# Triangular inverses in blocks of 16 instead of 8, with a planner that counts float32 products as two passes and new orders in both mixers

## The chip, the core and the metric

The kernel runs on one core of a Trainium2 chip. The metric is the device time of one execution in microseconds (us); the time quoted is the median of three runs.

## The reference, cut to what matters

The kernel computes a trunk of two layers on 512 tokens of width 1024. Each layer is a half-step SwiGLU feed-forward, a mixer, and another half-step feed-forward, each with a norm before and after.

```python
def macaron_layer(x, mixer, ...):
    x = x + 0.5 * rmsnorm(swiglu(rmsnorm(x, ffn1_pre_g), ffn1_w_in, ffn1_w_out), ffn1_post_g)
    x = x + rmsnorm(mixer(rmsnorm(x, mix_pre_g)), mix_post_g)
    x = x + 0.5 * rmsnorm(swiglu(rmsnorm(x, ffn2_pre_g), ffn2_w_in, ffn2_w_out), ffn2_post_g)
    return x

def rwkv7_step(S, inp):              # mixer of layer 0, 8 heads of 64, token by token
    r_t, w_t, k_t, v_t, kk_t, a_t = inp
    sa = einsum("bhvk,bhk->bhv", S, -kk_t)
    S = S * w_t[:, :, None, :] + einsum("bhv,bhk->bhvk", sa, kk_t * a_t) + einsum("bhv,bhk->bhvk", v_t, k_t)
    return S, einsum("bhvk,bhk->bhv", S, r_t)

# beside it in the same mixer: a gated linear recurrence h = a*h + u over 512 channels (RG-LRU)
# mixer of layer 1: stick-breaking attention, 16 heads of 64, blocks of 128 queries
```

## The kernel before

Activations lie transposed, channels on the 128 partitions and 512 tokens along the free axis. Each weight and each activation of a projection is split into a high and a low float32r part, and a projection is three products per tile (high by high, high by low, low by high), issued at L316 (`main`). A projection tile is 24 products of 128x512, or twice 24 of 128x256 where it is made for the two halves of the tokens apart. `nu` is how many tiles at a sub-layer's start, and `no` how many at its end, are made in halves, so that one half's norm runs while PE works on the other.

Layer 0's mixer (`Mixer0`, about 382 to 750 us of the span) runs the token recurrence in chunks of 64. The heads go in four pairs, and each pair passes through three threads. `pair` (L296) forms decays and scores. `inverse` (L297) inverts the 64x64 unit triangles, and `chain` (L298) carries the states and forms the output, which `result` (L302) splits for the output projection. The 16 triangles of a pair are inverted in two steps. First the diagonal 8x8 blocks are inverted on DVE: the blocks go through DRAM into `lane`, one block to a partition (128 partitions), and for t = 1 to 7 a multiplication over t*t elements and a sum over them (`TENSOR_REDUCE`) give row t. The thread `home` writes the result to DRAM (two DMAs) and reads it back as X and its transpose XT (four DMAs). Then PE doubles the block size at the levels 8, 16 and 32. A level is 16 products with X, a masked multiplication on DVE that gives Z, 32 products with Z, and two additions on DVE; the last level makes 16 products with Z and one addition. All of these are 64x64 float32 products, and each stands in the trace as two records.

Layer 1's mixer (`Mixer1`, about 1465 to 1740 us) is the attention: `group` and `head` (L309). Weights come by DMA from the queue SP: `weights` (L286), and `presplit` (L288), which stores the mixers' split weights in DRAM ahead of time.

Nothing of the order is written by hand. Threads are Python generators, and `Run` merges them: it keeps a clock for each engine, adds an estimated cost for each instruction (`matmul` and `vector`), and always emits the instruction that can start first by these clocks. Each engine then executes its instructions in the order in which they were emitted. The estimates so decide which instructions stand between two dependent ones. `HEAT`, `LIMIT`, `KEEP`, `PRIO`, `NAT`, `FLYING` and the like are limits and priorities of this merge. `BIAS` weighs GpSimd against DVE where either can run an elementwise operation.

The lines L280 to L317 in a trace are the table `CALLS`, one line for each thread: L280 `unit_ev`, L283 `out_ev`, L286 `weights`, L290 `low`, L291 `norm`, L296 `pair`, L297 `inverse`, L298 `chain`, L300 `rglru_tile`, L302 `result`, L303 `gate`, L309 `group`, L316 `main`, L317 `finish`.

Of the kernel before, what the change touches and what calls it, by code (L numbers as in the profile page):

```python
# [48 lines left out]
NAT = 2  # L49
# [10 lines left out]
def _consts():  # L60

    p = np.arange(P)
    j, t = p % 64, np.arange(64)
    out = {}
    out["scmask"] = np.concatenate([j[:, None] < t, j[:, None] <= t], 1)
    for b in (8, 16, 32):
        out[f"lv{b}"] = (j[:, None] // b % 2 == 1) & (t // b == j[:, None] // b - 1)
    out["reset"] = np.broadcast_to(np.arange(T) % 64 != 0, (P, T))
    out["eye2"] = j[:, None] == t
    out["blk2"] = np.stack([p < 64, p >= 64], 1)  # L70
    caus = np.where(p[None] < p[:, None], 0.0, -1e30)
    return out, {"caus": caus, "ones": np.ones((P, T))}
# [19 lines left out]
def _ffn_chunks(w_in, w_out):  # L92
# [11 lines left out]
    "wa k0 r0 v0 k1 r1 v1 g k2 r2 x0 x1 v2 k3 r3 x2 x3 v3 b0 b1 b2 b3").split()]  # L104
# [171 lines left out]
BIAS = 0.0  # L276
# [65 lines left out]
class Run:  # L342
# [39 lines left out]
    def matmul(self, op, w, x):  # L382

        n = math.prod(x.shape[1:])
        rows, cols = w.shape[0], math.prod(w.shape[1:])
        part, self.part = self.part, rows <= 64 or cols <= 64
        turn = 0.1 if part != self.part else 0.0
        if op == "transpose":
            return turn + 0.115 * max(w.shape[1], 64) / P
        if w.dtype == F32R:  # L390
            return turn + 0.012 + n / 2380.0
        if n <= 2:
            return 0.112
        if rows <= 64 and cols <= 64:
            return turn + (0.034 if n <= 64 else 0.056)
        if rows <= 64:
            return turn + 0.065 * max(n, P) / P
        if cols <= 64:
            return turn + (0.037 if n <= 64 else 0.073)
        return turn + 0.02 + 4 * n / 2380.0  # L400
# [616 lines left out]
class FFN(Sub):  # L1017
    nu, no = 6, 6
# [107 lines left out]
class Mixer0(Sub):  # L1126


    nu, no = 5, 4
# [257 lines left out]
    def inverse(self, p, AR, BK, SA, SR, rsc, bc, ec):  # L1387

        net, mm, tr, DA = self.net, self.net.PE.matmul, self.net.PE.transpose, self.net.run.DA
        V, S, G = net.V, net.S, net.G  # L1390
# [7 lines left out]
        lane, XL, tmp = yield from regs(64, P, 64)  # L1398
        lanes, back = Ev(), Ev()

        def out():
            for e in range(2):
                d1 = self.d1[p][8 - 8 * e : 16 - 8 * e, 0:4096].rearrange("k (j t) -> j k t", t=64)
                for g in range(2):
                    DA.dma_start(d1[:, g * 4 : g * 4 + 4], SAv[g][hh[1 - e], :, e])
            yield
            DA.dma_start(lane[:, 0:64].rearrange("l (j t) -> l j t", t=8),
                         self.d1[p].rearrange("k (b y) -> (k b) y", b=8)[:, 0:512].rearrange("l (j t) -> l j t", t=64)[:, :, 0:8])
# [3 lines left out]
        G.memset(XL[:, 0:64], 0.0)  # L1412
        G.memset(XL[:, 0:64:9], 1.0)
# [30 lines left out]
        xl = XL[:, 0:64].rearrange("l (j s) -> l s j", s=8)  # L1444
        for t in range(1, 8):
            tv = tmp[:, 0 : t * t].rearrange("l (s j) -> l s j", j=t)
            V.tensor_mul(tv, lane[:, t:64:8][:, 0:t].unsqueeze(1).to_broadcast([P, t, t]), xl[:, 0:t, 0:t])
            yield
            V.tensor_reduce(XL[:, 8 * t : 9 * t], tv, axis=AX.X, op=ALU.add)
            yield  # L1450
        S.copy(XL[:, 64:P].rearrange("l (s t) -> l s t", s=8), XL[:, 0:64].rearrange("l (t s) -> l s t", s=8))
# [4 lines left out]
        def home():  # L1456
            for m in range(2):
                d2 = self.d2[p][16 * m : 16 * m + 16].rearrange("k (b y) -> (k b) y", b=8)[:, 0:512]
                DA.dma_start(d2.rearrange("l (t s) -> l t s", s=64)[:, :, 0:8],
                             XL[:, 64 * m : 64 * m + 64].rearrange("l (t s) -> l t s", s=8))  # L1460
# [31 lines left out]
        for lv in (8, 16, 32):  # L1492
# [305 lines left out]
    def main(self):  # L1798
# [24 lines left out]
        order = (4, 5, 6, 7, 0, 1, 2, 3)  # L1823
# [12 lines left out]
class Mixer1(Sub):  # L1836


    nu, no = 4, 4
# [3 lines left out]
    FLYING = 4  # L1843
# [349 lines left out]
```

## Time and profile before

| what | value |
|---|---|
| median of three runs | 2120.53 us (2118.77 to 2123.96) |
| profiled execution | 2123.64 us, span 2121.9 us, mean granted clock 0.983 |
| PE busy | 2058.8 us, 97% of the span |
| DVE, ACT, POOL busy | 1213.1, 821.3, 148.2 us |
| `Mixer0` with its edges | about 382 to 750 us |
| `Mixer1` with its edges | about 1465 to 1765 us |

The four feed-forwards fill the rest of the span. A busy PE is not a PE at its peak: the ends of products are modelled and overlap. What one product costs is read from the starts of rows that follow each other without a wait.

### The profile page before, as it was taken

What the parts mean: (1) busy time and instruction counts of PE and PEld (TensorE: products, weight loads), DVE (VectorE), ACT (ScalarE), POOL (GpSimd) and SP (SyncE); (2) the same over time, 40 slices, a digit from 0 to 9 for tenths busy, and PEclk for the clock granted to TensorE, in tenths of its full rate; (3) what the DMA queues carried; (4) which work ended last, traced back from release to release, by engine and by line L of the source; (5) the groups of instructions that cost most, each with busy time, mean ns of one, the idle gap of its engine ahead of it and who ended that gap; (6) DMA issues with size and microseconds to landing.
All of it is one profiled execution on the core that took longest, in us unless ns stands there. A gap on an engine that the chain in (4) does not pass through costs nothing.

```text
span 2121.9 us, 30752 instructions
## 1 busy us (share of the span) xinstructions
PE 2058.8 (97%) x12392; PEld 1758.6 (83%) x12392; DVE 1213.1 (57%) x2091; ACT 821.3 (39%) x1332; POOL 148.2 (7%) x178
## 2 busy tenths in 40 slices
PE   8999999999998999999999999999999999999997
PEld 7888889877776888888898888888888788888887
DVE  6545455666684764545575343446698875344444
ACT  5343333442643444333443322223466543322221
POOL 0000000200110200000030000002111020000000
PEclk9999999999999999999999999999999999999999
DMA  5767666533243257667742322233233421322221
GB/s 177 267 243 257 238 259 215 201 116 93 87 129 133 90 195 261 250 238 257 256 149 83 116 99 99 91 106 120 100 119 120 179 90 53 117 99 91 98 80 40
DMA packets 118016, 319.00 MB, mean 150 GB/s; under 512 B 35569, under 2 KB 40305, under 8 KB 117873
## 3 DMA queue, kind: packets, MB, share of 16 engines
q1 hardware_dynamic: 117872, 317.03, 42.9%
q8 instruction: 97, 1.59, 0.3%
q14 instruction: 47, 0.38, 0.1%
HBM read 244.34 MB, written 72.65 MB: 149 GB/s over the span
## 4 chain that ended last, share of the span: by engine, by line
PE 58%; DVE 7%; issue 1%; POOL 1%; ACT 1%; POOLq 0%; DVEq 0%; ACTq 0%
PE bank L316 55%; PE bank L309 2%; DVE b L309 2%; DVE b L280 1%; DVE b L317 1%; DVE b L290 1%; DVE b L293 0%; DVE b L282 0%; PE bank L317 0%; PE bank L291 0%; POOL b L291 0%; DVE b L291 0%; DVE b L295 0%; ACT b L309 0%; DVE bank L309 0%
## 5 line engine op out<-in xcount | busy, mean ns | idle before, releaser
L316 PE MATMUL bank<-b,b 128*128 128x512 f32 (+1 forms) x4809 | 936.6, 352 | 13.2 <-DVE b L290 10.2
L316 PEld LDWEIGHTS bank<-b,b 128*128 128x128 f32 x4809 | 792.0, 191 | 134.1 <-DVE b L290 14.2
L316 PE MATMUL bank<-b,whi 128*128 128x512 f32 (+1 forms) x2872 | 809.6, 366 | 18.1 <-ACT b L302 7.0
L316 PEld LDWEIGHTS bank<-b,whi 128*128 128x128 f32 x2872 | 518.0, 192 | 101.2 <-ACT b L302 7.6
L316 PE MATMUL bank<-b,wlo 128*128 128x512 f32 (+1 forms) x1436 | 525.1, 366 | 0.8 <-DVE wlo L286 0.8
L280 DVE TENSOR_TENSOR b<-bank,b 128x512 f32<-128x512 f32 (+1 forms) x237 | 145.7, 620 | 435.1 <-PE bank L316 430.6
L316 PEld LDWEIGHTS bank<-b,wlo 128*128 128x128 f32 x1436 | 275.7, 192 | 42.9 <-issue 1.9
L286 ACT CAST whi<-wraw 128x1024 fp32r<-128x1024 f32 (+2 forms) x121 | 121.5, 1005 | 292.4 <-PE bank L316 249.6
L286 ACT CAST b<-wraw 128x1024 fp32r<-128x1024 f32 (+1 forms) x154 | 157.2, 1023 | 196.1 <-PE bank L316 161.7
L286 DVE TENSOR_TENSOR b<-wraw,b 128x1024 fp32r<-128x1024 f32 (+1 forms) x154 | 183.1, 1189 | 61.6 <-ACT b L286 61.3
L286 DVE TENSOR_TENSOR wlo<-wraw,whi 128x1024 fp32r<-128x1024 f32 (+2 forms) x121 | 140.8, 1165 | 50.0 <-ACT whi L286 50.0
L280 ACT CAST b<-b 128x512 fp32r<-128x512 f32 (+3 forms) x160 | 88.8, 557 | 174.5 <-DVE b L280 173.2
L282 DVE TENSOR_TENSOR b<-bank,b 128x256 f32<-128x256 f32 (+1 forms) x88 | 47.9, 544 | 151.9 <-PE bank L316 151.9
L280 DVE TENSOR_TENSOR b<-b,b 128x512 fp32r<-128x512 f32 (+5 forms) x170 | 106.1, 627 | 8.3 <-ACT b L280 5.3
L317 POOL TENSOR_TENSOR b<-b,power 128x2 f32<-128x2 f32 x12 | 11.1, 928 | 1407.2 <-DVE b L317 1076.5
L280 ACT ACTIVATE b<-b 128x512 f32<-128x512 f32 (+1 forms) x100 | 57.2, 577 | 109.7 <-DVE b L280 109.7
L288 DVE TENSOR_TENSOR b<-b,b 128x1024 f32<-128x1024 f32 x62 | 75.5, 1220 | 6.2 <-ACT b L288 6.2
L288 ACT CAST b<-b 128x1024 fp32r<-128x1024 f32 x62 | 64.5, 1044 | 5.9 <-DMA b<-in_w_dram 5.9
L282 ACT ACTIVATE b<-b 128x256 f32<-128x256 f32 (+1 forms) x56 | 25.0, 447 | 107.2 <-DVE b L282 107.2
L289 ACT ACTIVATE b<-b,par 128x256 fp32r<-128x256 f32 x96 | 46.7, 500 | 43.1 <-POOL b L293 30.2
L297 PEld LDWEIGHTS bank<-b,b 64*64 64x64 f32 x1264 | 44.1, 136 | 10.6 <-issue 5.4
L290 DVE SCALAR_TENSOR_TENSOR b<-b,par,b 128x256 fp32r<-128x256 f32 x96 | 52.1, 553 | 0.3 <-ACT b L289 0.2
(170 smaller groups left out, 1562.5 us busy)
## 6 DMA issues: line engine op xcount, KB each, us to landing
wraw<-in_w_dram SPq DMA_DIRECT2D x240, 512.0 KB, 3.3
parts<-b SPq DMA_DIRECT2D x124, 512.0 KB, 3.9
b<-in_w_dram SPq DMA_DIRECT2D x62, 512.0 KB, 4.8
wlo<-parts SPq DMA_DIRECT2D x47, 512.0 KB, 3.5
whi<-parts SPq DMA_DIRECT2D x47, 512.0 KB, 4.5
b<-parts SPq DMA_DIRECT2D x30, 512.0 KB, 5.4
wraw<-in_w_dram SPq DMA_DIRECT2D x32, 384.0 KB, 3.0
rwkv_inverses<-b SPq DMA_DIRECT2D x4, 520.0 KB, 4.0
```

The costliest lines, as they stand in the source:

```text
L280: "unit_ev": lambda f, a, k: f(*a, **k),
L282: "third_ev": lambda f, a, k: f(*a, **k),
L286: "weights": lambda f, a, k: f(*a, **k),
L288: "presplit": lambda f, a, k: f(*a, **k),
L289: "pre": lambda f, a, k: f(*a, **k),
L290: "low": lambda f, a, k: f(*a, **k),
L297: "inverse": lambda f, a, k: f(*a, **k),
L309: "group": lambda f, a, k: f(*a, **k),
L316: "main": lambda f, a, k: f(*a, **k),
L317: "finish": lambda f, a, k: f(*a, **k),
```

## The change

The diagonal blocks are 16x16. There are 64 of them in a pair, on 64 partitions, and t runs from 1 to 15 instead of 7, so the DVE part has 30 instructions in place of 14. PE doubles at the levels 16 and 32 only. The DMAs of a pair are as many as before (four writes of the scores, one read into `lane`, two writes and four reads in `home`), in pieces of 16x16 instead of 8x8.

The merge's estimates for small float32 products are about twice what they were. Limits and priorities differ: `HEAT` is 0, which turns off a rule that held back projections; `NAT` is 1, so one pair of buffers for attention weights instead of two; `FLYING` is 6. `Mixer0` makes six tiles in halves at its start instead of five, and `Mixer1` five at its end instead of four. The order of `Mixer0`'s projection tiles and of its output's inputs differs.

```diff
-KEEP = (3, 8, 8)
+KEEP = (3, 6, 8)
-RGN = 2
+RGN = 4
-WPRIO = 5
-HEAT = 4000
+WPRIO = 4
+HEAT = 0
-MLIMIT = {"m": 3, "b": 5}
+MLIMIT = {"m": 4, "b": 4}
-NAT = 2
+NAT = 1
...
-    "wa k0 r0 v0 k1 r1 v1 g k2 r2 x0 x1 v2 k3 r3 x2 x3 v3 b0 b1 b2 b3").split()]
+    "wa r0 v0 g k0 k1 r1 v1 r2 k2 x0 x1 v2 k3 r3 v3 x2 x3 b0 b1 b2 b3").split()]
...
-BIAS = 0.0
+BIAS = 0.2
...
         if n <= 2:
-            return 0.112
+            return 0.2
         if rows <= 64 and cols <= 64:
-            return turn + (0.034 if n <= 64 else 0.056)
+            return turn + (0.064 if n <= 64 else 0.115)
         if rows <= 64:
-            return turn + 0.065 * max(n, P) / P
+            return turn + 0.13 * max(n, P) / P
         if cols <= 64:
-            return turn + (0.037 if n <= 64 else 0.073)
+            return turn + (0.05 if n <= 64 else 0.13)
...
 class Mixer0(Sub):
-    nu, no = 5, 4
+    nu, no = 6, 4
...
-        xl = XL[:, 0:64].rearrange("l (j s) -> l s j", s=8)
-        for t in range(1, 8):
-            tv = tmp[:, 0 : t * t].rearrange("l (s j) -> l s j", j=t)
-            V.tensor_mul(tv, lane[:, t:64:8][:, 0:t].unsqueeze(1).to_broadcast([P, t, t]), xl[:, 0:t, 0:t])
+        xl = XL[0:64, 0:256].rearrange("l (j s) -> l s j", s=16)
+        for t in range(1, 16):
+            tv = tmp[0:64, 0 : t * t].rearrange("l (s j) -> l s j", j=t)
+            V.tensor_mul(tv, lane[0:64, t:256:16][:, 0:t].unsqueeze(1).to_broadcast([64, t, t]), xl[:, 0:t, 0:t])
             yield
-            V.tensor_reduce(XL[:, 8 * t : 9 * t], tv, axis=AX.X, op=ALU.add)
+            V.tensor_reduce(XL[0:64, 16 * t : 17 * t], tv, axis=AX.X, op=ALU.add)
             yield
...
-        for lv in (8, 16, 32):
+        for lv in (16, 32):
...
-        order = (4, 5, 6, 7, 0, 1, 2, 3)
+        order = (6, 5, 4, 7, 0, 1, 2, 3)
...
 class Mixer1(Sub):
-    nu, no = 4, 4
+    nu, no = 4, 5
-    FLYING = 4
+    FLYING = 6
```

What the merge makes of it is shown at three places on PE.

The first place is the start of `Mixer0`. The order on PE before, from the second product of the decays of pair 0 (L296, three products of 64 partitions by 512) to the small sums (128x2) that need a long stretch of DVE work behind the decays:

```order
L296 MATMUL bank_82<-b_39_2369,b_52_2597 128x512 x2
L296 MATMUL bank_82<-b_39_2369,b_38_1487 128x512
L316 MATMUL bank_87<-b_49_2594,whi_80 128x256
...
L316 MATMUL bank_86<-b_38_1487,whi_76 128x512
...
L316 MATMUL bank_86<-b_51_2596,whi_76 128x512
L296 MATMUL bank_83<-b_43_2549,b_23_264 128x2 x4
L296 MATMUL bank_83<-b_43_2549,b_44_2562 128x2 x4
```

The same stretch in the changed kernel, with the products of `gate` (L303) in it:

```order
L296 MATMUL bank_84<-b_39_2369,b_52_2597 128x512 x2
L296 MATMUL bank_84<-b_39_2369,b_38_1487 128x512
L303 MATMUL bank_86<-b_54_3179,b_37_1421 128x512 x3
L316 MATMUL bank_82<-b_51_2596,b_26_353 128x256
...
L303 MATMUL bank_85<-b_54_3179,b_37_1421 128x512 x3
L303 MATMUL bank_87<-b_54_3179,b_37_1421 128x512 x3
L316 MATMUL bank_89<-b_38_1487,whi_76 128x512
...
L316 MATMUL bank_83<-b_36_764,wlo_79 128x512
L296 MATMUL bank_88<-b_43_2549,b_27_392 128x2 x4
L296 MATMUL bank_88<-b_43_2549,b_16_143 128x2 x4
```

Before, 3 products of 256 columns and 17 of 512 stand between; now 9 of `gate`, 5 of 256 columns and 39 of 512.

The second place is the fourth inverse. The order on PE before, where the output projection (L316 with `bank_86`, `bank_87` and others) has begun and the levels 8 and 16 run (X first as the moving input of 16 products, then 32 products with Z in two banks):

```order
L297 MATMUL bank_88<-b_4_93,b_58_3835 64x64 x8
...
L297 MATMUL bank_85<-b_57_3675,b_4_93 64x64 x16
L297 MATMUL bank_89<-b_4_93,b_57_3675 64x64 x16
...
L316 MATMUL bank_86<-b_36_764,whi_80 128x512
L297 MATMUL bank_88<-b_4_93,b_64_4808 64x64 x8
L297 MATMUL bank_88<-b_4_93,b_58_3835 64x64 x8
L316 MATMUL bank_86<-b_33_588,whi_80 128x512
...
L297 MATMUL bank_84<-b_57_3675,b_4_93 64x64 x16
L297 MATMUL bank_85<-b_4_93,b_57_3675 64x64 x16
```

The order now, from the last product of the third chain (L298) through level 16 to level 32:

```order
L298 MATMUL bank_84<-b_60_3787,b_57_3591 64x64
L297 MATMUL bank_82<-b_63_5027,b_3_92 64x64 x8
L297 MATMUL bank_82<-b_63_5027,b_59_3786 64x64 x8
L297 MATMUL bank_87<-b_46_2588,b_63_5027 64x64 x16
L297 MATMUL bank_83<-b_63_5027,b_46_2588 64x64 x16
L316 MATMUL bank_86<-b_49_2594,whi_78 128x512 x2
...
L297 MATMUL bank_87<-b_63_5027,b_3_92 64x64 x8
L297 MATMUL bank_87<-b_63_5027,b_59_3786 64x64 x8
L297 MATMUL bank_83<-b_63_5027,b_46_2588 64x64 x16
```

Level 8 is gone, level 16 stands ahead of the output projection's first product, and nothing stands any more between a level's products with X and those with Z.

The third place is the end of `Mixer1`. The order on PE before, from the broadcast product of `finish` for the first half (L317), through the second half's output tiles, to the first product of the next feed-forward (`bank_82`):

```order
L317 MATMUL bank_84<-b_114_10373,ones 128x256
L316 MATMUL bank_85<-b_121_11089,b_118_10794 128x256
...
L316 MATMUL bank_87<-b_120_11047,b_48_2593 128x256
L316 MATMUL bank_87<-b_123_11360,b_138_13085 128x256
L316 MATMUL bank_82<-b_77_5809,b_135_12807 128x256
```

The same stretch now; the next feed-forward begins with `bank_88`:

```order
L317 MATMUL bank_84<-b_133_10630,ones 128x256
L316 MATMUL bank_86<-b_117_9259,b_136_10699 128x256
...
L316 MATMUL bank_85<-b_145_12172,whi_76 128x256
L316 MATMUL bank_85<-b_123_9885,wlo_77 128x256
L316 MATMUL bank_88<-b_142_11393,whi_78 128x256
```

Before, 63 products of 256 columns stand between the two; now 77.

## Rows read from the trace of the kernel before

**Rows 1.** The page: each engine's busy time in us, share of the span, instructions.
```profile
PE 2058.8 (97%) x12392; PEld 1758.6 (83%) x12392; DVE 1213.1 (57%) x2091; ACT 821.3 (39%) x1332; POOL 148.2 (7%) x178
```

**Rows 2.** Windows by stage: PE, PEld, DVE, ACT, POOL busy us, clock, DMA, GB/s.
```profile
850.00:900.00 50.00, 50.00 (x222) 41.39 (x221) 30.08 (x34) 18.30 (x22) 0.00 (x0) 1.00 0.67 244
437.00:592.00 155.00, 155.00 (x1779) 121.22 (x1780) 103.80 (x277) 70.26 (x120) 15.15 (x19) 0.99 0.35 103
631.00:690.00 59.00, 50.28 (x577) 36.56 (x576) 30.91 (x53) 24.57 (x43) 3.72 (x4) 0.91 0.43 136
1497.00:1697.00 200.00, 192.49 (x1185) 167.43 (x1184) 165.20 (x325) 115.17 (x246) 28.17 (x32) 1.00 0.37 137
```

**Rows 3.** Timeline of PE, products of the fourth inverse: start, us, instruction, records.
```profile
649.17 2.13 PE L297 MATMUL bank<-b,b 64*64 64x64 f32 x64
651.23 0.50 PE L316 MATMUL bank<-b,wlo 128*128 128x512 f32 x1
...
653.03 1.20 PE L297 MATMUL bank<-b,b 64*64 64x64 f32 x32
654.16 0.72 PE L316 MATMUL bank<-b,whi 128*128 128x512 f32 x2
```

**Rows 4.** Timeline of PE, 256-column products back to back.
```profile
1752.71 5.80 PE L316 MATMUL bank<-b,b 128*128 128x256 f32 x47
```

**Rows 5.** Lines on PE, 400 to 438 us: busy, mean ns, idle before and releaser.
```profile
L316 PE MATMUL bank<-b,b 128*128 128x256 f32 x48 | 9.8, 362 | 2.0 <-DVE b L290 2.0
```

**Rows 6.** Timeline of PE at pair 0: decay product, then the sums that wait.
```profile
421.62 0.96 PE L296 MATMUL bank<-b,b 64*128 64x512 f32 x3
...
431.56 1.87 PE L296 MATMUL bank<-b,b 128*128 128x2 f32 x8 [3.74 <-DVE b L296]
```

**Rows 7.** Windows around three falls of the granted clock, columns as in rows 2.
```profile
400.00:438.00 38.00, 32.24 (x189) 28.42 (x188) 21.44 (x56) 15.36 (x29) 2.99 (x4) 0.82 0.40 145
631.00:698.00 67.00, 55.39 (x589) 40.32 (x589) 35.51 (x60) 28.72 (x48) 3.72 (x4) 0.87 0.37 120
1725.00:1766.00 41.00, 36.12 (x253) 34.43 (x253) 33.14 (x79) 21.40 (x49) 17.18 (x20) 0.88 0.15 52
```

**Rows 8.** Lines on PE, 631 to 698 us, those with idle time before them.
```profile
L316 PE MATMUL bank<-b,whi 128*128 128x512 f32 x48 | 20.4, 489 | 8.9 <-ACT b L302 7.0 <-DVE b L302 1.0 <-DMA whi<-parts 0.9
L298 PE MATMUL bank<-par,b 128*128 128x128 f32 x8 | 1.3, 282 | 2.7 <-DVE b L298 2.7
```

**Rows 9.** Timeline of PE: 30 products of the fourth chain, and its end.
```profile
681.04 2.42 PE L298 MATMUL bank<-b,b 128*64 128x64 f32 x60
...
692.89 1.52 PE L316 MATMUL bank<-b,whi 128*128 128x512 f32 x2 [2.97 <-ACT b L302]
```

**Rows 10.** Lines on DVE, shapes of the block inverse and a level's product.
```profile
L297 DVE TENSOR_TENSOR b<-bank,b 128x512 f32<-128x512 f32 x40 | 27.3, 689 | 23.8 <-PE bank L297 23.5
L297 DVE TENSOR_REDUCE b<-b 128x7 f32<-128x49 f32 x4 | 0.8, 199 | 0.0
L297 DVE TENSOR_TENSOR b<-b,b 128x49 f32<-128x49 f32 x2 | 0.5, 256 | 0.0
L297 DVE TENSOR_TENSOR b<-b,b 128x1 f32<-128x1 f32 x2 | 0.3, 152 | 0.0
```

**Rows 11.** Timeline of DVE and PE: the fourth inverse, first step to first level product.
```profile
622.54 0.15 DVE L297 TENSOR_TENSOR b<-b,b 128x1 f32<-128x1 f32 x1
...
630.76 0.19 DVE L297 TENSOR_REDUCE b<-b 128x7 f32<-128x49 f32 x1
...
631.01 1.20 PE L297 MATMUL bank<-b,b 64*64 64x64 f32 x32
...
640.74 2.03 PE L297 MATMUL bank<-b,b 64*64 64x64 f32 x32
```

**Rows 12.** Lines on PE, 1725 to 1766 us, those with idle time before them.
```profile
L316 PE MATMUL bank<-b,b 128*128 128x256 f32 x155 | 23.2, 304 | 2.8 <-DVE b L290 2.7
L291 PE MATMUL bank<-b,ones 128*128 128x256 f32 x4 | 1.3, 404 | 2.1 <-DVE b L291 2.1
```

More of the change, by code (lines that the diff above doesn't have):

```diff
@@ L65, in _consts @@
     out["scmask"] = np.concatenate([j[:, None] < t, j[:, None] <= t], 1)
-    for b in (8, 16, 32):
+    for b in (16, 32):
         out[f"lv{b}"] = (j[:, None] // b % 2 == 1) & (t // b == j[:, None] // b - 1)
@@ L1397, in inverse @@
             yield ev["a2", p - A2N, "done"]
-        lane, XL, tmp = yield from regs(64, P, 64)
+        lane, XL, tmp = yield from regs(256, 512, 256)
         lanes, back = Ev(), Ev()
@@ L1406, in out @@
             yield
-            DA.dma_start(lane[:, 0:64].rearrange("l (j t) -> l j t", t=8),
-                         self.d1[p].rearrange("k (b y) -> (k b) y", b=8)[:, 0:512].rearrange("l (j t) -> l j t", t=64)[:, :, 0:8])
+            DA.dma_start(lane[0:64].rearrange("l (j t) -> l j t", t=16),
+                         self.d1[p].rearrange("k (b y) -> (k b) y", b=4)[:, 0:1024].rearrange("l (j t) -> l j t", t=64)[:, :, 0:16])
             net.run.set(lanes)
         net.run.spawn(out(), 0)
-        G.memset(XL[:, 0:64], 0.0)
-        G.memset(XL[:, 0:64:9], 1.0)
+        G.memset(XL[0:64, 0:256], 0.0)
+        G.memset(XL[0:64, 0:256:17], 1.0)
         yield ev["v", p]
@@ L1443, in inverse @@
         yield lanes
-        xl = XL[:, 0:64].rearrange("l (j s) -> l s j", s=8)
-        for t in range(1, 8):
-            tv = tmp[:, 0 : t * t].rearrange("l (s j) -> l s j", j=t)
-            V.tensor_mul(tv, lane[:, t:64:8][:, 0:t].unsqueeze(1).to_broadcast([P, t, t]), xl[:, 0:t, 0:t])
+        xl = XL[0:64, 0:256].rearrange("l (j s) -> l s j", s=16)
+        for t in range(1, 16):
+            tv = tmp[0:64, 0 : t * t].rearrange("l (s j) -> l s j", j=t)
+            V.tensor_mul(tv, lane[0:64, t:256:16][:, 0:t].unsqueeze(1).to_broadcast([64, t, t]), xl[:, 0:t, 0:t])
             yield
-            V.tensor_reduce(XL[:, 8 * t : 9 * t], tv, axis=AX.X, op=ALU.add)
+            V.tensor_reduce(XL[0:64, 16 * t : 17 * t], tv, axis=AX.X, op=ALU.add)
             yield
-        S.copy(XL[:, 64:P].rearrange("l (s t) -> l s t", s=8), XL[:, 0:64].rearrange("l (t s) -> l s t", s=8))
+        S.copy(XL[0:64, 256:512].rearrange("l (s t) -> l s t", s=16), XL[0:64, 0:256].rearrange("l (t s) -> l s t", s=16))
         XX = yield from regs(2 * T)
@@ L1457, in home @@
             for m in range(2):
-                d2 = self.d2[p][16 * m : 16 * m + 16].rearrange("k (b y) -> (k b) y", b=8)[:, 0:512]
-                DA.dma_start(d2.rearrange("l (t s) -> l t s", s=64)[:, :, 0:8],
-                             XL[:, 64 * m : 64 * m + 64].rearrange("l (t s) -> l t s", s=8))
+                d2 = self.d2[p][16 * m : 16 * m + 16].rearrange("k (b y) -> (k b) y", b=4)[:, 0:1024]
+                DA.dma_start(d2.rearrange("l (t s) -> l t s", s=64)[:, :, 0:16],
+                             XL[0:64, 256 * m : 256 * m + 256].rearrange("l (t s) -> l t s", s=16))
             yield
```

## Prediction

> **What bounds the kernel now.** I read the page first: PE is busy for 97% of the span and DVE for 57% [rows 1]. Then windows by stage. In a feed-forward PE is never idle, and 222 products of 512 columns take 50 us, so one costs 0.225 us [rows 2]; nothing there can move but PE work, and the change makes none. The mixers differ. From 437 to 592 us PE is full as well, but from 631 to 690 us it idles for 8.7 of 59 us at a clock of 0.91 [rows 2]: the fourth inverse and chain, with little left to put between their steps. In the attention's middle PE idles for 7.5 of 200 us and DVE is busy for 165 [rows 2]. Third, the lines of three short stretches, to see who ended PE's waits [rows 5, 8, 12], and the granted clock there [rows 7]. So the time is PE work plus waits at the mixers' edges, and each wait costs again when the clock falls to its lower level behind it.
>
> **The change part by part.** I make the sum against the profiled execution's own time, 2123.6 us; its span is 2121.9, and it lies 3.1 us above the median of the three runs.
>
> *Level 8 goes.* That is 16 + 32 products in each of four pairs. Sixteen products (32 records) take 1.13 us from their start to the next product's, thirty-two take 2.06 [rows 3]. Together 3.19 us a pair, 12.8 us for four. PE was full around three of the four, so this is on the path: **-12.8**.
>
> *Two more tiles in halves.* 48 products of 512 columns become 96 of 256. The latter cost 0.120 us (47 in 5.80, less about 0.16 of the last one's tail) [rows 4]: 96 x 0.120 - 48 x 0.225 = **+0.7**.
>
> *DVE's blocks.* No row shows a block of 16, so I carry the rows of 8 on. A multiplication takes 152 ns for 1 element and 256 for 49, or 2.1 ns an element; a sum takes 199 ns at 49, about 1 ns an element [rows 10]. The squares of 1 to 15 add up to 1240, so 30 instructions take 30 x 0.15 + 1240 x 0.0031 = 8.4 us, with 35 ns between them 9.4. Before, 14 took 2.9. That is +6.5 a pair; the three 512-wide products of a level give 2.1 back [rows 10]. Net 18 us of DVE work, over a stretch where DVE is busy for 104 of 155 us: it is hidden as work. As lateness it is not. Before, the 14 steps of the fourth inverse spread from 622.54 to 630.95, since other work stands between them, and X could first be used 9.7 us after the products that follow the steps (631.01 to 640.74: DRAM and back) [rows 11]. In the changed order, from those 16 products to the first level-16 product, I count for pairs 0 to 3 PE work of 10.3, 7.5, 9.9 and 7.3 us at the prices of the rows (for the fourth: 1.1 for the 16 products themselves, nine of 512 columns at 0.225, 30 chain products at 2.4 [rows 9], about 1.8 for the rest). Two are short of 9.7 by over 2 us. Below: nothing, if DVE is early. Above: 6 us a pair, with the clock, 25 us. I take the shortfall of the middle pairs with one fall of the clock: **+6**.
>
> *The start of `Mixer0`.* PE waits 2.0 us for the second half's norm [rows 5] and 3.7 us at 431.56, where sums of pair 0 wait for DVE [rows 6]; the clock is 0.82 of full, which costs 32.2 busy us x 0.18 = 5.8 [rows 7]. Together 11.5. Now one more half tile, 24 x 0.12 = 2.9 us, covers the norm. The path of the second wait is 9.9 us long (421.62 to 431.56). Before, 3 x 0.12 + 17 x 0.225 = 4.2 us of products stood in it; now 9 of 512 columns, 5 of 256 and 39 of 512 make 11.4. The sixth half tile also adds work on DVE ahead of the norm. Bounds 0 and -11.5; I take **-8**.
>
> *The tail of `Mixer0`.* Waits of 8.9 and 2.7 us [rows 8], and a clock of 0.87 over 55.4 busy us, 7.2 [rows 7]; 18.8 in all. What is late is the fourth pair. Its level 16 now stands ahead of the output projection, all gate inputs are done before it, and level 8 is out of the chain. The last wait, 2.97 us for the split of the fourth output [rows 9], stays with its slow clock. New ones come where nothing stands between X's and Z's products: about 1 us for each of two levels, and up to 2.4 before X. Bounds 0 and -16; I take **-9**.
>
> *The end of `Mixer1`.* Waits of 2.7 and 2.1 us [rows 12], the clock 0.88 over 36.1 busy us, 4.3 [rows 7]; 9.1. The fifth tile in halves puts 24 more products, 2.9 us, between the first half's last output and the next feed-forward. Bounds 0 and -9; I take **-5**.
>
> *The middle of `Mixer1`.* One attention buffer instead of two, six groups in flight. In both orders a head's transposes stand behind the head before it, so the second buffer is hardly used. I take 0, with -5 and +8 as bounds, the 7.5 us of idle time there [rows 2] removed or doubled.
>
> The sum is -12.8 + 0.7 + 6 - 8 - 9 - 5 = -28.1, or 2095.5; with some of the profiled execution's 3.1 us taken off, **2094 us**.
>
> A stretch of small products has a price of its own: two of sixteen take 2 x 1.13 us, one of thirty-two 2.06 [rows 3], so 0.20 us is spent at a stretch's two edges. [...]
>
> **The rivals.**
>
> *Waits move.* Only the PE work comes off: the waits of the start and the tail turn up between X and Z. 2123.6 - 12.1 = 2111.5. For it: PE executes in order, and the new estimates put less between dependent steps. Against it: the two long waits each have a named cover now.
>
> *It does not do what it says.* The products saved are given back by the steps that come late, about 3 us a pair: 2120. For it: before, PE was full beside three of the four inverses [rows 2], so a late step cost nothing there; with less PE work the same step shows. Against it: 12.1 us of work would have to turn into waits where there was none.
>
> *Slower.* The thirty steps stretch as the fourteen did, 8.4 for 2.9 us, to 27 us a pair, and every instruction on DVE behind them waits too: norm inputs, bank evictions, pair sums. If each inverse comes 10 us later than its place in the order, that is 40 us, and four falls of the clock at 2.9 (half of the start's 5.8, which holds two) add 12: 2123.6 - 34.1 + 52 = 2142. Its terms are the sum's -34.1 without the +6. It decides from about 8 us a pair with the clock, which takes back all that is gained. For it: 152 ns for one element [rows 10] make sixteen more small instructions dear. [...] Against it: in the new order 8 to 18 us of other DVE work already stands between the steps, so their stretch is planned for, and PE has work before them.
>
> **How the numbers follow.** The forecast's own range is 2082 to 2108. Forecast 0.57, waits move 0.17, does not do what it says 0.13, slower 0.13. A measurement of this kernel tells 0.3%, or 6.4 us, from no change. The forecast and most of the first rival lie below 2114; the rest of that one and the second lie within 0.3%. Faster 0.70, same 0.17, slower 0.13. The range leaves out the worst of the slow case and the ends where all gains come at their bounds: 2076 to 2117.
>
> **What would show it.** 384 fewer 64x64 records at L297; 120 steps on DVE of up to about 0.6 us; no wait over 1 us at pair 0's sums; the fourth chain's last wait some 25 us earlier against the mixer's start; no clock below full between 1725 and 1766 us. The prediction is wrong if PE waits for DVE at L297 by more than 6 us a pair, if the clock falls between 450 and 600 us, or if the attention's middle grows by over 8 us.

## Result and profile after

The changed kernel takes 2069.17 us (median of 4 runs, 2066.37 to 2069.47), the kernel before 2120.89 on the same chip: a ratio of 0.9752, 95% interval 0.9735 to 0.9769. It is faster by 51.7 us. The forecast was 2094 with a range of 2076 to 2117: the sign was right, the time lies 7 us below the range, and the gain is about twice what was forecast. The profiled executions differ by 54.3 us of span, 2121.9 and 2067.6.

The page of the changed kernel, engines' rows (against [rows 1]):

```profile
PE 2024.6 (98%) x12056; PEld 1739.0 (84%) x12056; DVE 1214.7 (59%) x2148; ACT 817.1 (40%) x1329; POOL 150.0 (7%) x177
```

PE has 336 records fewer, 384 of 64x64 gone and 48 more from the halved tiles, as counted. DVE is as busy as it was, though it has 57 instructions more.

Windows of the changed kernel over the stages of [rows 2, 7], columns as there:

```profile
376.00:438.00 62.00, 61.58 (x441) 56.28 (x440) 39.74 (x108) 26.62 (x53) 8.55 (x13) 1.00 0.49 181
432.00:592.00 160.00, 158.34 (x1634) 122.84 (x1635) 136.20 (x388) 79.31 (x135) 22.29 (x27) 0.98 0.37 111
592.00:655.00 63.00, 55.83 (x613) 42.69 (x612) 37.18 (x72) 25.77 (x46) 9.36 (x8) 0.96 0.42 141
655.00:710.00 55.00, 51.56 (x380) 49.92 (x379) 45.61 (x97) 28.68 (x59) 16.33 (x19) 0.92 0.33 111
800.00:850.00 50.00, 50.00 (x222) 41.39 (x221) 27.63 (x32) 18.20 (x22) 0.00 (x0) 1.00 0.65 235
1455.00:1655.00 200.00, 197.29 (x1224) 174.11 (x1223) 164.36 (x332) 117.55 (x250) 29.51 (x30) 1.00 0.37 132
1672.00:1718.00 46.00, 45.24 (x368) 44.38 (x367) 42.41 (x95) 28.52 (x57) 16.91 (x20) 1.00 0.32 104
```

A feed-forward is what it was: 222 products in 50 us. The gain is at the edges. The start of `Mixer0` (first row) now has 0.4 us of idle time at full clock, where before there were 5.8 us at 0.82 from 400 us on [rows 7]; the end of `Mixer1` (last row) has 0.8 us at full clock, where before 4.9 at 0.88 [rows 7]. The attention's middle idles for 2.7 us instead of 7.5 [rows 2].

Timeline of PE at pair 0's sums in the changed kernel, the place of [rows 6]:

```profile
415.64 0.96 PE L296 MATMUL bank<-b,b 64*128 64x512 f32 x3
...
417.93 1.55 PE L303 MATMUL bank<-b,b 128*128 128x512 f32 x6
...
427.93 0.39 PE L316 MATMUL bank<-b,wlo 128*128 128x512 f32 x1
428.16 1.84 PE L296 MATMUL bank<-b,b 128*128 128x2 f32 x16
```

The sums start 12.5 us after the decays without a wait; before it was 9.9 us, 3.74 of them idle.

Timeline of DVE and PE at the fourth inverse, the place of [rows 11]:

```profile
575.50 0.15 DVE L297 TENSOR_TENSOR b<-b,b 64x1 f32<-64x1 f32 x1
...
595.79 0.54 DVE L297 TENSOR_TENSOR b<-b,b 64x225 f32<-64x225 f32 x1
...
596.44 0.37 DVE L297 TENSOR_REDUCE b<-b 64x15 f32<-64x225 f32 x1
...
598.22 1.09 PE L297 MATMUL bank<-b,b 64*64 64x64 f32 x30
...
605.47 1.20 PE L297 MATMUL bank<-b,b 64*64 64x64 f32 x32
609.57 3.65 PE L297 MATMUL bank<-b,b 64*64 64x64 f32 x64 [2.90 <-DVE b L297]
```

The thirty steps stretch over 21 us here (14.6, 27.7 and 18.9 in the other pairs), of which DVE works on them for 7.7 us. The first level's products with X (605.47) do not wait, 7.25 us after the start of the products that follow the steps (598.22); nor does any product with X wait at this level in the other three pairs. Those with Z wait 2.90 us for the DVE product between them, the new kind of wait that the prediction named (it said about 1 us).

**A table by stage.** The runs below are read by one measure. For each product I take the time from its start to the next one's start. Its price is the median of its shape in the two traces (33 ns for a 64x64 record, from [rows 3]). What it took above the price is lost: a wait, a slow clock, or a change of tile shape (0.19 us each in e2). The table holds one profiled execution of each kernel. Priced so, the work went from 1999.2 to 1987.1 us, the lost time from 107.2 to 64.8. The stages: the first 35 us; the start of `Mixer0` from the last feed-forward sum to the first inverse's first product; the next 155 us; from there to 50 us past the first half's sum in its output; the attention from its first to its last product; and from there to 35 us past the second half's sum. The rest (boundaries of feed-forwards, start of `Mixer1`, end of the program) lost 17.7 us before and 16.7 after. How far two executions of one order differ can be read from the table too: e11, e15 and e16 have the changed kernel's order until 1480 us or later, and in the first four stages they differ from it by up to 1.2 us; e1 has the order of the kernel before in the first 35 us and differs there by 3.1 us. One run each of e14 and e15 took 2876.62 and 4478.19 us, far from their other three, and is left out below.

```
lost us                  program  Mixer0  next    Mixer0    attention  end of
                         start    start   155 us  late,end  middle     Mixer1
before                   10.1     15.3    10.1    29.5      13.7       10.8
after                     4.5      1.9    12.7    20.2       7.1        1.7
e1 blocks only            7.0     12.3    10.7    44.9      14.5       10.1
e2 estimates only         7.8     13.1    43.4    41.1      14.1       10.8
e8 blocks + estimates     9.7     11.2    13.4    35.6      13.9       10.7
e3 after, blocks of 8     4.7      2.0     7.1    24.9       7.1        1.7
e4 after, old estimates   5.9      2.0    16.0    41.7       7.0        7.4
e5 after, old Mixer1      4.1      2.0    16.4    29.0      18.6        6.4
e6 after, old Mixer0      4.7     11.8    11.4    22.9       7.1        1.6
e7 after, old limits      6.6      2.7    12.7    28.6      10.4        8.3
e9 after, BIAS 0          6.4      2.7    14.0    23.3      10.1        8.7
e10 after, HEAT 4000      4.5      1.8    12.7    23.7       7.0        1.6
e11 after, NAT 2          4.3      2.0    11.7    20.7       9.5        2.3
e12 after, old banks      5.2      2.0    13.1    26.4       9.6        1.7
e13 after, nu 5           4.2      6.0    15.7    28.4       7.1        1.6
e14 after, old order      4.1      7.7    10.8    30.9       6.9        1.6
e15 after, no 4           4.2      1.9    13.9    21.3      13.2        7.3
e16 after, FLYING 4       4.1      2.0    12.7    19.9      12.2        6.7
e17 after, dearer 64x64   4.9      1.9    17.2    22.3       7.1        1.7
e18 after, BIAS 0.4       4.8      1.5    16.5    28.4       9.6        7.4
```

### The profile page after: what moved, and what is told of

It reads as the page before. It is cut to its first block, busy times and chain, and to the rows that moved or that the text cites. A ratio compares the mean times of both kernels' runs of the same rounds, so it can differ in the third digit from the quotient of the medians.

```text
span 2067.6 us, 30121 instructions
## 1 busy us (share of the span) xinstructions
PE 2024.6 (98%) x12056; PEld 1739.0 (84%) x12056; DVE 1214.7 (59%) x2148; ACT 817.1 (40%) x1329; POOL 150.0 (7%) x177
## 4 chain that ended last, share of the span: by engine, by line
PE 72%; issue 17%; DVE 8%; ACT 2%; POOL 1%; DMA 0%; POOLq 0%; SPq 0%; DVEq 0%; ACTq 0%
PE bank L316 64%; PE bank L309 2%; DVE b L309 2%; PE bank L297 2%; PE bank L298 1%; DVE b L317 1%; PE bank L296 1%; DVE b L280 1%; DVE b L290 1%; DVE b L282 1%; DVE b L293 1%; PE bank L291 1%; PE bank L317 0%; DVE b L291 0%; PE bank L300 0%
## 5 line engine op out<-in xcount | busy, mean ns | idle before, releaser
L316 PE MATMUL bank<-b,b 128*128 128x512 f32 (+1 forms) x4802 | 929.8, 350 | 8.5 <-DVE b L290 7.0
L316 PEld LDWEIGHTS bank<-b,b 128*128 128x128 f32 x4802 | 787.3, 190 | 126.7 <-DVE b L290 8.2
L316 PE MATMUL bank<-b,whi 128*128 128x512 f32 (+1 forms) x2908 | 807.7, 362 | 12.1 <-ACT b L289 6.3
L316 PEld LDWEIGHTS bank<-b,whi 128*128 128x128 f32 x2908 | 520.4, 191 | 92.8 <-ACT b L289 6.3
L316 PE MATMUL bank<-b,wlo 128*128 128x512 f32 (+1 forms) x1454 | 526.6, 362 | 0.8 <-DVE wlo L286 0.8
L316 PEld LDWEIGHTS bank<-b,wlo 128*128 128x128 f32 x1454 | 277.3, 191 | 40.8 <-issue 1.3
L317 POOL TENSOR_TENSOR b<-b,power 128x2 f32<-128x2 f32 x12 | 11.1, 926 | 1384.5 <-DVE b L317 1384.5
L309 DVE TENSOR_TENSOR_SCAN b<-b,b 128x512 f32<-128x512 f32 (+1 forms) x64 | 50.8, 827 | 0.3
L290 DVE SCALAR_TENSOR_TENSOR b<-b,par,b 128x256 fp32r<-128x256 f32 x96 | 50.6, 536 | 0.2 <-ACT b L289 0.2
```

Of the source, the lines that this page charges most:

```text
L290: "low": lambda f, a, k: f(*a, **k),
L309: "group": lambda f, a, k: f(*a, **k),
L316: "main": lambda f, a, k: f(*a, **k),
L317: "finish": lambda f, a, k: f(*a, **k),
```

## Experiments

My theory A: PE work of 12 us goes with level 8, and the rest of the gain is waits and slow clock that another order of the same instructions takes away. The rival B: the shorter inverse itself frees the mixer's tail, and the numbers of the merge do little. Each ratio is to the kernel before on the same chip, whose median lay between 2120.1 and 2122.2.

**e1, the blocks alone**, on the kernel before:

```diff
-        for lv in (8, 16, 32):
+        for lv in (16, 32):
...
-        for t in range(1, 8):
+        for t in range(1, 16):
```

(and all other lines of the diff in `inverse` and the table of masks).

> The kernel before with blocks of 16 alone (estimates, limits and orders as before). Theory A (the gain of the whole change is mostly waits that the new order takes away, and the blocks give only their PE work): 12.8 us of products gone, some 6 to 10 us of it given back where X comes late, since the old estimates leave room for 14 DVE steps and not for thirty: 2112 to 2120, and the wait of 3.7 us at pair 0's sums and those at the end of Mixer1 stay. Theory B (the shorter inverse is what frees Mixer0's tail): 2120.9 - 12.8 - about 9 of the tail = 2099 or less.

2123.42 us, ratio 1.0009 (1.0000 to 1.0019): nothing gained, 3 us above A's range. The work is 12.7 us less, the late part loses 15.4 more. Lines on PE, 592 to 686 us of e1, those with most idle time before them (columns as in [rows 5]):

```profile
L316 PE MATMUL bank<-b,whi 128*128 128x512 f32 x78 | 32.1, 476 | 13.6 <-ACT b L302 10.8 <-DVE b L302 2.9
...
L297 PE MATMUL bank<-b,b 64*64 64x64 f32 (+1 forms) x224 | 9.4, 229 | 3.0 <-DVE b L297 3.0
...
L298 PE MATMUL bank<-par,b 128*128 128x128 f32 x16 | 3.9, 388 | 3.2 <-DVE b L298 3.2
```

The output projection waits for `result` (L302), as before [rows 8], and longer: 13.6 us instead of 8.9. No product of e1 waits for X, so the way in which A expected the loss did not come about. Why `result` comes later here is not shown. B falls.

**e2, the estimates alone**, and **e8, blocks and estimates**, on the kernel before:

```diff
         if n <= 2:
-            return 0.112
+            return 0.2
         if rows <= 64 and cols <= 64:
-            return turn + (0.034 if n <= 64 else 0.056)
+            return turn + (0.064 if n <= 64 else 0.115)
```

(with the two other pairs of estimates of the diff; e8 has the blocks of 16 as well).

> The kernel before with the merge's new estimates for small float32 products alone. Theory A: no product goes, but threads are placed better in Mixer0; its start and tail lose part of their 30 us of waits and slow clock: 2105 to 2116. The first feed-forward and Mixer1, which hold few such products, hardly change. Theory B (estimates are worth nothing without the blocks): 2118 to 2124.

> The kernel before with blocks of 16 and the new estimates, nothing else. Blocks alone gave nothing and estimates alone cost 36 us. If the two only add: 2120 + 3 + 36 = 2156 to 2160. If the estimates are what leaves room for thirty DVE steps: 2100 to 2125, with the late part of Mixer0 at 20 us of lost time instead of 35.

e2: 2156.47 us, ratio 1.0164 (1.0120 to 1.0209), outside both expectations: 36 us slower. Its four executions lie apart: 2164.57 and 2164.87 us at a mean granted clock of 0.972, 2148.36 and 2145.94 us at 0.981 and 0.982. The trace is of the first. e8: 2115.19, ratio 0.9978 (0.9968 to 0.9989), inside the second expectation, though its late part loses 35.6 us and not the 20 expected. They don't add: on top of the new estimates the blocks are worth 31 to 50 us, by which execution of e2 is taken. Where the traced execution of e2 loses most is 482 to 530 us. Timeline of PE just before, and a window over it:

```profile
469.97 0.50 PE L316 MATMUL bank<-b,whi 128*128 128x512 f32 x1
470.40 0.32 PE L297 MATMUL bank<-b,b 64*64 64x64 f32 x2
470.65 0.50 PE L316 MATMUL bank<-b,wlo 128*128 128x512 f32 x1
```

```profile
450.00:482.00 32.00, 32.00 (x244) 23.38 (x242) 16.33 (x47) 11.51 (x22) 1.55 (x3) 1.00 0.41 118
482.00:530.00 48.00, 48.00 (x244) 29.14 (x243) 13.87 (x45) 5.98 (x10) 0.00 (x0) 0.50 0.11 31
```

Here the merge lays single products of 512 columns and single ones of 64x64 in turn. From start to start the large one takes 0.43 us, the small one 0.25, against 0.227 in a row of its kind and 0.07: 0.19 us per change of tile shape. Then the clock is at 0.50 of full for 48 us, though PE is never idle. The other pair of executions was 16 to 19 us faster; a mean clock that is higher by 0.009 over some 2150 us means, as an estimate, about 40 us less at half clock, so they were without most of this stretch. The 36 us are a middle between 26 and 45.

**e3, blocks of 8, and e4, old estimates**, on the changed kernel (the two diffs above, turned round):

> The changed kernel with blocks of 8 and three levels again. Theory A: the 12.2 us of PE work come back, the waits for the thirty DVE steps (about 8 us between 592 and 655 us) partly go: 2069.2 + 12.2 - 4 = 2077, between 2072 and 2085; start of the program, start of Mixer0 and all of Mixer1 stay as after. Theory B: the tail's waits return as well, 2090 or more.

> The changed kernel with the old estimates for small float32 products. Theory A: threads in Mixer0 stand too close, X and the sums are waited for more: 2069.2 + 8 to 20 = 2077 to 2090, all of the loss between 380 and 700 us. Theory B (the limits and orders of threads do it, not the estimates): within 5 us of 2069.

e3: 2082.21, ratio 0.9819 (0.9804 to 0.9833), in A's range: 13.0 us slower than the changed kernel. 12.7 us of work come back; the 155 us lose 5.6 less, the late part 4.7 more, so the blocks cost about 1 us of lost time in all. e4: 2099.06, ratio 0.9894 (0.9878 to 0.9911), 29.9 us slower, more than expected, 21.5 of it late in `Mixer0`; 5.7 are at the end of `Mixer1`, where nothing was expected. Lines on PE of e4, 585 to 690 us, those that wait for the inverse, its chain and the sums:

```profile
L298 PE MATMUL bank<-b,b 128*64 128x64 f32 (+2 forms) x288 | 16.1, 250 | 7.4 <-DVE b L298 5.7 <-DVE b L297 1.0 <-ACT b L298 0.7
L297 PE MATMUL bank<-b,b 64*64 64x64 f32 (+1 forms) x312 | 14.7, 251 | 6.8 <-DMA b<-rwkv_inverses 6.0 <-DVE b L297 0.8
...
L298 PE MATMUL bank<-par,b 128*128 128x128 f32 x24 | 4.8, 353 | 5.2 <-DVE b L298 5.2
L297 PE MATMUL bank<-par,b 128*128 128x128 f32 x24 | 4.5, 305 | 5.7 <-DVE b L296 2.6 <-DVE b L298 2.0 <-ACT b L297 1.1
```

A's direction holds for both, its size for e3 alone: the blocks give their PE work in the changed kernel's order and give nothing in that of e1. In e4 PE does wait for X, 6.0 us for the DMA of `rwkv_inverses`. In the changed kernel `chain` (L298) does not wait here and `inverse` (L297) waits less (592 to 655 us):

```profile
L316 PE MATMUL bank<-b,whi 128*128 128x512 f32 x66 | 23.6, 424 | 3.2 <-ACT b L302 3.0 <-DVE b L302 0.2
...
L297 PE MATMUL bank<-b,b 64*64 64x64 f32 x192 | 8.4, 252 | 4.0 <-DVE b L297 4.0
...
L298 PE MATMUL bank<-b,b 128*64 128x64 f32 x148 | 5.9, 228 | 0.0
```

**e5, e6, e7: the other numbers in groups**, each set back in the changed kernel. For e5:

```diff
-MLIMIT = {"m": 4, "b": 4}
+MLIMIT = {"m": 3, "b": 5}
-NAT = 1
+NAT = 2
-    nu, no = 4, 5
+    nu, no = 4, 4
-    FLYING = 6
+    FLYING = 4
```

For e6, which has the old `M0_UNITS` too:

```diff
-    nu, no = 6, 4
+    nu, no = 5, 4
-        order = (6, 5, 4, 7, 0, 1, 2, 3)
+        order = (4, 5, 6, 7, 0, 1, 2, 3)
```

For e7:

```diff
-KEEP = (3, 6, 8)
+KEEP = (3, 8, 8)
-RGN = 4
+RGN = 2
-WPRIO = 4
-HEAT = 0
+WPRIO = 5
+HEAT = 4000
-BIAS = 0.2
+BIAS = 0.0
```

> The changed kernel with Mixer1's side as before: two pairs of attention buffers, four groups in flight, four output tiles in halves, and the old limits on banks for the mixers. Theory A (these settings took the waits of Mixer1): the 6.6 us of its middle and the 9.1 us of its end come back, 2069.2 + 15.7 = 2085, between 2079 and 2090; Mixer0 as after. Theory B (Mixer1 gains from what reaches it earlier, the limits elsewhere): 2067 to 2073.

> The changed kernel with the old order of Mixer0's projections and of its output's inputs, and five tiles in halves. Theory A: the 3.7 us wait at pair 0's sums and the slow clock at the start come back, 13 us, and some of the late part: 2080 to 2095. Theory B (the estimates and limits placed them): 2066 to 2075.

> The changed kernel with the old priorities and limits that hold for all stages (projections held back by HEAT, WPRIO 5, two regions, KEEP 8, no BIAS). Theory A: the start of the program gets its second wait and slow clock back, 5 us, and Mixer0 is placed differently, 0 to 10 us: 2074 to 2085. Theory B (these numbers do nothing): 2066 to 2072.

e5: 2093.73, ratio 0.9875 (0.9853 to 0.9896); the attention and its end lose 16 us more, as expected, and `Mixer0` 12 more, which was not, so the time lies above A's range. e6: 2082.10, ratio 0.9828 (0.9812 to 0.9845), in A's range, 9.9 of it at the start of `Mixer0`. e7: 2091.89, ratio 0.9875 (0.9858 to 0.9892), slower than expected: 8.4 us late in `Mixer0`, 6.6 at `Mixer1`'s end, 3.3 in the attention and 2.1 at the program's start.

**e9 to e16: one number each**, set back in the changed kernel: BIAS 0; HEAT 4000; NAT 2; MLIMIT 3 and 5; nu 5; the old `M0_UNITS`; no 4; FLYING 4 (the lines stand in the diff above and in that of the change).

> The changed kernel with BIAS 0 again (the margin by which GpSimd must be earlier than DVE before it gets an operation that either can do). KEEP, RGN and WPRIO at their old values leave the order of all engines' instructions as it is, so of the limits for all stages only BIAS and HEAT can act. BIAS acts from the first microseconds on. Theory A (BIAS took away the second wait of the start): lost time at the start 7 instead of 4.5 us, Mixer0 and Mixer1 placed differently by a few us each way: 2070 to 2082. Theory B (HEAT alone makes the 22.7 us of all limits together): within 4 us of 2069.

> The changed kernel with HEAT 4000 again, the rule that holds projections back while PE has done little. It acts only in the late part of Mixer0. Theory A: projections held back leave less between the fourth pair's steps, the late part loses 18 to 22 us instead of 12.6: 2073 to 2081, and Mixer1 stays within 3 us. Theory B: within 4 us of 2069.

> The changed kernel with two pairs of attention buffers. The order differs only in Mixer1, from its middle on. Theory A (as predicted, the second buffer is hardly used): 2065 to 2073. Theory B (two buffers let a later head's transposes come ahead of what is due, and the middle's 6.6 us of waits come back): 2074 to 2082.

> The changed kernel with at most 3 banks for projections and 5 for the rest in the mixers, as before, instead of 4 and 4. Theory A (a fourth bank lets a projection stand where a small product would wait): late part of Mixer0 20 to 23 us of lost time instead of 12.6, Mixer1's middle 12 to 18 instead of 7.1, so most of the 24.5 us of the run with all of Mixer1's settings: 2082 to 2094. Theory B (the attention's own settings made that difference): 2067 to 2075.

> The changed kernel with five tiles in halves at Mixer0's start instead of six. Theory A (the order of the projections covers pair 0's sums, the half tile only the norm): the start of Mixer0 loses 2 to 5 us instead of 1.9, the long wait at the sums stays away: 2069 to 2076. Theory B (the half tile covers both): 10 to 13 us lost at the start, 2078 to 2084.

> The changed kernel with the old order of Mixer0's projections, all else as after. Theory A: the sums of pair 0 wait for DVE again, by 3.4 to 4.7 us as in every run with the old order so far, and the clock falls behind: 10 to 13 us lost at the start of Mixer0, 2077 to 2084. Theory B: under 4 us lost there, 2067 to 2073.

> The changed kernel with four output tiles in halves at Mixer1's end instead of five. Theory A (the 2.9 us of products cover the next feed-forward's norm): 6 to 10 us lost at Mixer1's end instead of 1.6, 2073 to 2078. Theory B (what comes earlier from the middle covers it): 2066 to 2071.

> The changed kernel with four groups of attention in flight instead of six. Two buffers instead of one cost 2 us and the old bank limits 2.5 us of Mixer1's middle, and all of its settings together 11.5. Theory A (the groups in flight make the larger part): the middle loses 11 to 18 us instead of 7.1, 2073 to 2081. Theory B: it loses 7 to 9, 2068 to 2072.

```
                     us        ratio (95% interval)
e9  BIAS 0           2085.20   0.9832 (0.9813 to 0.9852)
e10 HEAT 4000        2072.62   0.9776 (0.9756 to 0.9796)
e11 NAT 2            2070.92   0.9768 (0.9750 to 0.9785)
e12 MLIMIT 3, 5      2080.47   0.9811 (0.9793 to 0.9830)
e13 nu 5             2083.91   0.9820 (0.9800 to 0.9840)
e14 old M0_UNITS     2083.03   0.9812 (0.9779 to 0.9845)
e15 no 4             2080.61   0.9803 (0.9777 to 0.9829)
e16 FLYING 4         2078.84   0.9797 (0.9777 to 0.9818)
```

e10 and e11 are not told apart from the changed kernel (0.9735 to 0.9769); the six others are slower. Theory A came true in e11, in e16 and, by its time, in e14; B came true in e10. e9 and e15 took longer than A said, though the loss that A named came (6.4 us at the program's start, 7.3 at `Mixer1`'s end). e12 lies between the two. e13 has B's time, but its start loses 6.0 us, which neither named. `KEEP`, `RGN` and `WPRIO`, each set back alone or all three together, give the same program, so they do nothing here. The order of the output's inputs and each single estimate were not set back alone.

The start of `Mixer0` has two causes that add: the sixth half tile (e13, 4.1 us more lost there) and the order of the projections (e14, 5.8 more); both together, e6, 9.9. They do not add over the whole: late in `Mixer0` e13 loses 8.2 us more and e14 10.7, and e6, which has both and the old order of the output's inputs, only 2.7. In e14 pair 0's sums wait again:

```profile
413.24 0.96 PE L296 MATMUL bank<-b,b 64*128 64x512 f32 x3
...
420.13 0.95 PE L296 MATMUL bank<-b,b 128*128 128x2 f32 x8
424.00 0.37 PE L296 MATMUL bank<-b,b 128*128 128x2 f32 x1 [2.92 <-DVE b L296]
```

e15's row of 1686 to 1732 us, the end of `Mixer1`, and its lines:

```profile
1686.00:1732.00 46.00, 42.95 (x320) 41.50 (x320) 38.62 (x86) 25.17 (x55) 16.48 (x19) 0.93 0.19 64
```

```profile
L316 PE MATMUL bank<-b,b 128*128 128x256 f32 x205 | 27.9, 290 | 3.1 <-DVE b L290 2.8
```

The wait for the next feed-forward's norm (L290) is back without the fifth half tile. But e15 also loses 6.1 us more in the attention, and e16 5.1 there and 5.0 at the end: each of these numbers changes the order in more places than its own (e15's differs from 1634 us on, still in the attention). Lines on PE of the attention, those with most idle time before them, first of the kernel before (1497 to 1697 us), then of the changed kernel (1455 to 1655 us):

```profile
L309 PE MATMUL bank<-par,b 128*128 128x128 f32 x160 | 28.7, 278 | 5.0 <-DVE b L309 4.3 <-POOL b L309 0.6
```

```profile
L309 PE MATMUL bank<-par,b 128*128 128x128 f32 x160 | 26.7, 273 | 0.6 <-DVE b L309 0.6
L309 PE MATMUL bank<-b,b 128*128 128x512 f32 x64 | 21.8, 409 | 1.4 <-DVE b L309 0.9 <-ACT b L309 0.5
```

With four groups in flight (e16, 1455 to 1666 us) the attention's products wait again:

```profile
L309 PE MATMUL bank<-b,b 128*128 128x512 f32 x64 | 22.7, 423 | 5.2 <-ACT b L309 2.8 <-DVE b L309 2.4
```

BIAS moves residual additions (L293) between the engines: in the changed kernel 46 stand on GpSimd and 42 on DVE, in e9 49 and 39, before 50 and 38. Source L293 of the changed kernel: engine, count, least, median and most ns, times of the first and the last:

```profile
L293 POOL TENSOR_TENSOR b<-b,b x46: 722/740/940, 363.7 to 2043.5; 128x256 f32<-128x256 f32 x46
L293 DVE TENSOR_TENSOR b<-b,b x42: 409/414/965, 367.4 to 2045.6; 128x256 f32<-128x256 f32 x42
```

Three additions at 0.33 us more each are 1 us; the 16 us of e9 are in the waits of the other order (table), not in the additions.

**e17 and e18: a step further**, on the changed kernel:

```diff
-            return turn + (0.064 if n <= 64 else 0.115)
+            return turn + (0.08 if n <= 64 else 0.14)
```

```diff
-BIAS = 0.2
+BIAS = 0.4
```

> The changed kernel with the estimate of a 64x64 product a quarter higher (0.08 and 0.14 instead of 0.064 and 0.115). Theory A (a higher price leaves more room before X): late part of Mixer0 under 10 us of lost time, 2062 to 2068. Theory B (each value only draws another order): 2069 to 2085, with new waits in Mixer0's late part.

> The changed kernel with BIAS 0.4 instead of 0.2; BIAS 0 cost 16 us. Theory A (fewer operations on the slower GpSimd are better): 2060 to 2068. Theory B (each value only draws another order): 2069 to 2085.

e17: 2076.42, ratio 0.9792 (0.9778 to 0.9807). e18: 2086.58, ratio 0.9832 (0.9816 to 0.9849). Both are slower than the changed kernel, as their counterparts on the other side are: A of these two falls, and B holds (e18 lies 1.6 us above its range). No version here beats the changed kernel.

## Why the prediction fell short

The sum was -28.1; by the table the profiled executions differ by -12.1 of work and -42.4 of lost time, 26.4 more than the sum. The PE work was right. What failed are terms for waits and slow clock, and all in one direction: two things were put at nothing, the middle of `Mixer1` (-6.6 measured, beyond its own bound of -5) and the program's start (-5.6); the start of `Mixer0` and the end of `Mixer1` were taken at 8 of 11.5 and 5 of 9 us and gave 5.4 and 4.1 more; and the +6 for a late X was paid for a wait that did not come (3.4). Step by step:

- **Level 8 and the halves**, -12.1: measured -12.1 of priced work, and 12.7 between e3 and the changed kernel (blocks alone). Right.
- **DVE's blocks**, +6: measured +2.6 in the 155 us, and by e3, which takes the blocks alone, 5.6 more there and 4.7 less later. The steps cost DVE 7.7 us a pair, 8.4 was worked out. They stretched to as much as 27.7 us, just as the slower rival said, and that cost little. The wait that was priced, X late by up to 2.4 us, did not come in any pair: the fourth pair's X was used 7.25 us after the products that follow the steps, without a wait, so the 9.7 us of [rows 11] were not the least it takes. (The pairs with too little work, 7.5 and 7.3 us, were also the second and the fourth, not the middle two.) Lost in the 155 us are about 3.4 us to a half clock without a wait (below) and 1.7 us of other waits at `inverse`. X was late only in e4. e1 loses 15 us late in `Mixer0`, where `result` is waited for and not X. "It does not do what it says" came true there in its time, and not in the whole change.
- **Start of `Mixer0`**, -8 of at most -11.5: measured -13.4. The waits were read right: 5.8 us idle before, none after. The bound was too small by its clock term: two stretches of 6.8 us at half clock (0.51 of full over 404 to 411 us, 0.53 over 431 to 438) cost up to 6.8 us, where 5.8 was worked out; what is left, about 1 us, is spread over many products. The two covers that the prediction named, the half tile and the longer row behind the decays, are the causes (e13, e14).
- **Tail of `Mixer0`**, -9: measured -9.3. Right in sum, and in part by luck. The last wait for `result` stayed, 2.97 us at 652.08 us, as said; the waits before products with Z were 4.0 us in the fourth inverse instead of about 2; and PE waits 3.4 us for the next feed-forward's norm instead of 2.0, which had no term. Line on PE of the changed kernel, 655 to 710 us:

```profile
L316 PE MATMUL bank<-b,b 128*128 128x256 f32 (+1 forms) x282 | 38.4, 293 | 3.4 <-DVE b L290 2.0 <-ACT b L289 1.4
```

- **End of `Mixer1`**, -5: measured -9.1. Mis-sized: the fifth half tile is worth 5.6 there (e15), but four in flight, old estimates or another BIAS lose as much there (e16, e4, e9, e18).
- **Middle of `Mixer1`**, 0 between -5 and +8: measured -6.6, the largest miss. The argument looked at one edit, the second buffer, and was right that it does little there (e11, 2.4 us). It priced six groups in flight at nothing; set back alone, they cost 5.1 there (e16). What else the merge places anew by its other numbers had no term: the fifth output tile in halves 6.1 (e15), BIAS 3.0 (e9), the bank limits 2.5 (e12). These add up to more than 6.6 and do not divide it.
- **The program's start**, no term: -5.6. "In a feed-forward PE is never idle" was read from 850 to 900 us and carried to the first 35 us, where PE waits for weights. Windows of 0 to 35 us, before and in the changed kernel:

```profile
0.00:35.00 35.00, 25.05 (x154) 24.06 (x155) 24.15 (x56) 23.35 (x50) 3.19 (x8) 0.90 0.61 203
```

```profile
0.00:35.00 35.00, 27.82 (x199) 26.99 (x200) 26.29 (x63) 25.20 (x53) 3.93 (x8) 1.00 0.66 215
```

  A wait of 1.98 us for weights at 27.55 us is gone; with BIAS 0 it is back (1.74 us), and BIAS makes 1.9 of the 5.6 (e9). Up to 3.1 of the rest is luck of the execution: in the same order there e1 lost 7.0 and the kernel before 10.1, the latter at a clock of 0.90 (first row).

Of what was to show the steps, the records, the DVE steps, the free sums of pair 0 and the full clock at `Mixer1`'s end came as said. The fourth chain's last wait came 34 us earlier against the mixer's start, where 25 was said. The clock did fall between 450 and 600 us, which was named as a sign of failure; 6.8 us at half speed are in the 12.7 lost, and it came without a wait (below). As a sign it was badly chosen: before the change the clock is already at 0.50 for 3.4 us there, from 509.9 us, with PE busy throughout [rows 2].

Of the rivals, "waits move" (2111.5) would have left the lost time at 107 us; it fell to 65. With each term at its best bound (0 for the blocks, -11.5, -16, -9, -5) the prediction's own sum is -53.6, or 2070 us; its range left that end out, and the measured time is near it, though partly by other terms. The deeper error is that the change was summed as parts. Setting back one part at a time costs 13.0 (e3), 29.9 (e4), 16.0, 3.4, 1.8, 11.3, 14.7, 13.9, 11.4 and 9.7 us (e9 to e16), 125 in all, against 52 for the whole; blocks alone give 0 and estimates alone lose 26 to 45. The waits that went are shown. Why a given number draws the order that has none of them stays open; for two of the numbers a step to either side draws a worse one.

## What to carry to other kernels

Where a table of estimates and limits draws the order, its numbers have no price of their own: read the waits in the order that comes out, at every edge of every stage, the program's start among them. Work taken off a full engine is a gain only in an order that does not give it back as waits: the same edit of the blocks gave 0 us in one order and 13 in another. A gain from such numbers is a fit; after the next edit it has to be made anew.

## What was not expected of the hardware

The clock fell without a wait. In the traced execution of e2 PE was busy throughout 450 to 562 us, and its clock was at 0.50 of full from 482 to 530 us, and at 1.00 from 450 to 482 and from 530 to 562. Ahead of the fall, as its timeline shows from 469.39 to 472.84 us, PE alternated single 512-column products with one to three 64x64 products. The changed kernel shows it in little; windows of 485 to 500 and 500.4 to 507.2 us:

```profile
485.00:500.00 15.00, 15.00 (x169) 12.09 (x166) 13.44 (x45) 4.97 (x11) 0.53 (x1) 1.00 0.19 71
500.40:507.20 6.80, 6.80 (x26) 3.83 (x26) 4.83 (x14) 3.96 (x6) 0.00 (x0) 0.50 0.26 91
```

PE had no idle time ahead of this fall either; it ran the chain's small products between single large ones. So the prediction's picture, a fall of the clock behind each wait, is not the whole one. What sets it off in such a stretch was not tried by itself and stays open; by the mean clock, two of e2's four executions of the same program were without most of it.

A change of tile shape cost 0.19 us in that alternation. What the time goes into is not shown. The trace of the kernel before has 173 such changes in `Mixer0`, that of the changed kernel 147. The time of the 26 fewer is inside the lost time: as an estimate, at 0.10 us each, half of the 0.20 that [rows 3] give for a stretch's two edges, they would be 2.6 of the 42.4 us, at 0.19 us 4.9.
